# Attention's last output weights in buffers of their own, and the seventh tile's squares alone in the mean

## The chip, the core and the metric

The kernel is one program on one core of a Trainium2 chip. The metric is the device time of one launch in microseconds (us). A core has a matrix engine (PE in the profile), a vector engine (DVE), a scalar engine (ACT), a pool engine (POOL) and a queue that issues the large loads (SP). Each engine runs its instructions strictly in its own order and waits where an operand or a buffer is not ready; the engines work beside each other. Tiles live in on-chip memory of 128 partitions; matrix products go to eight accumulator banks of 512 columns.

## The reference

Two transformer layers over 256 tokens of width 1024, everything in 32-bit floats. Layer 0 mixes tokens by a mixture of three causal, dilated attentions with 16 heads, layer 1 by a gated linear attention in chunks. Both are followed by a gated feed-forward with a short convolution, and every sub-layer is normed and modulated by a conditioning vector. The part around the change:

```python
def rmsnorm(x, g):
    x32 = x.astype(jnp.float32)
    y = x32 * lax.rsqrt(jnp.mean(x32 * x32, axis=-1, keepdims=True) + EPS)
    return (y * g.astype(jnp.float32)).astype(x.dtype)
...
    return o.reshape(B, S, A_WIDTH).astype(h.dtype) @ w_out
...
        x = x + g1 * y
        h = rmsnorm(x, norm_ffn[i]) * (1.0 + sc2) + sh2
        x = x + g2 * conv_ffn(h, w_up[i], conv_w[i], conv_b[i], w_down[i])
```

## The kernel before

Activations are kept transposed: `x` is eight tiles of 128 channels by 256 tokens. Every product of 32-bit numbers is made as three products of a faster 32-bit form: each operand is split into a high part and a remainder, and `mm3` (lines 175 to 177) multiplies high by high, low by high and high by low. For a weight block `split` (line 155 on) loads the block into a raw buffer (one of four, tag `raw`), ACT rounds it to the high part `whi` in two halves (line 165), and DVE subtracts that from the raw block, again in two halves, which gives `wlo` (line 169). The pool `wspl` holds three buffers each of `whi` and `wlo`, so the fourth block in a row can be cast only when the last product that reads the first one is done.

Layer 0's attention goes over eight pairs of heads. For one pair `attend` makes the scores (tile `s`), adds the bias (`prob`, line 435), exponentiates (line 444), norms (`pn`, lines 450 and 451), transposes on PE (tile `t`, line 455), copies the result (`pt`, line 456), multiplies by the values (`po`, lines 460 and 464) and splits the result into `ohi` and `olo` (lines 469 and 470), one operand pair of 128 channels. `evacuate` takes queries and keys out of their banks (q on ACT, line 479; k on DVE, line 480).

`project` then multiplies the eight operand pairs by the output weights. It goes over four blocks n = 0 to 3 of 2048 columns; each block gives two output tiles (i = 0, 1), so 48 products `py` of 128x256. The last operand pair comes out of the last pair of heads; the products with the first seven need not wait for it. Block n has its own split weights, and the fourth one's reuse the first one's buffers. After a block `residual` adds its two tiles into `x` (DVE, line 322), `add_square` squares them on ACT (`sq`, line 199) and sums the squares (`sqacc`, line 202, tiles 0 to 2 on POOL, the rest on DVE), and `scale` makes `early_x` on ACT (line 287). `sums[0]` ends as the sum over tiles 0 to 6, `sums[1]` is tile 7 alone.

Then `all_normed` starts the feed-forward: products `early` of `early_x` with a first weight block (line 302), tiles 0 and 1 ahead of the mean; `rstd_of` multiplies `sums[0]` and `sums[1]` by a matrix of 1/1024 into one bank (tile `ms`, line 187), which is the mean over channels; ACT turns it into a reciprocal root (`ln`, `rstd`); the other six `early` products are put behind the `ms` products on PE; DVE and ACT make `xr`, `hhi` and `hlo` per tile, and PE goes on with the products `pab` of the feed-forward. The `early`, `ms`, `t` and `po` products use the slower, plain 32-bit form, and each of the first two shows as two records.

The order of the instructions on each engine is chosen when the kernel is built: a scheduler orders them by a timing model of its own under the data dependencies and buffer counts. `behind(...)` (and `issue_after`) adds an edge that keeps an instruction behind another one on the same engine. The order is fixed in the program after that; it does not react to what happens on the chip.

Of the kernel before, what the change touches and what calls it, by code (L numbers as in the profile page):

```python
# [57 lines left out]
def trunk(ctx: ExitStack, tc: tile.TileContext, I, out):  # L58
# [112 lines left out]

    def mm3(ps, a, b, start, stop):


        mm(ps, a[0], b[0], start=start, stop=False)  # L175
        mm(ps, a[0], b[1], start=False, stop=False)  # L176
        return mm(ps, a[1], b[0], start=False, stop=stop)  # L177
# [18 lines left out]
    def add_square(kt):  # L196
# [8 lines left out]
        part = 2 if kt < 3 else kt // 7  # L205
        if kt in (0, 3, 7):
            sums[part] = sq
        else:
            add(part, sq)
# [3 lines left out]
        if kt < 6:  # L213
            squared[0] = i

# [80 lines left out]
    def all_normed(l, sub, tag, early):  # L296
# [9 lines left out]
        r = rstd_of([sums[0], sums[1]], tag="p")  # L306
# [12 lines left out]
    def residual(l, sub, kt, ps):  # L319
        g = mod[l, 3 * sub + 2, kt]  # L320
        with behind(*(last_sum if kt == 7 else ())):
            i = last_x[kt // 7] = nc.vector.scalar_tensor_tensor(x[kt], ps, g[:, 0:1], x[kt], op0=ALU.mult, op1=ALU.add)
# [82 lines left out]

    def attend(u, q, k, v, bias):
# [32 lines left out]
        for h in range(2):  # L439
            rs = slice(2 * h, 2 * h + 2)  # L440
            nc.vector.tensor_scalar(m[:, 4:8][:, rs], m[:, 0:4][:, rs], -1.0, None, op0=ALU.mult)
            for r in (2 * h, 2 * h + 1):
                c = prob[r][:, 0 : KEYS + r]
                nc.scalar.activation(c, c, AF.Exp, bias=m[:, 4 + r : 5 + r], accum_out=m[:, 8 + r : 9 + r])
            nc.vector.reciprocal(m[:, 12:16][:, rs], m[:, 8:12][:, rs])
            for r in (2 * h, 2 * h + 1):
# [4 lines left out]
                nc.vector.tensor_scalar(pn[:, T:KEYS], prob[r][:, T + r : KEYS + r], f, None, op0=ALU.mult)  # L451
                t = bank("t", "t")
                for j in range(3):
                    c = slice(P * j, P * j + P)
                    nc.tensor.transpose(t[:, c], pn[:, c], ident)
                (nc.vector.tensor_copy if r % 2 else nc.scalar.copy)(pt[:, r, :], t[:, 0:KEYS])
# [4 lines left out]
        for r in range(4):  # L461
            for hh, e in enumerate(heads):
                at = P * (r % 2) + P + E * hh
                mm(po[e, CH * r : CH * r + CH], v[r // 2][:, at : at + E],
# [9 lines left out]
    def evacuate(q, k, g, pq, pk):  # L474
# [3 lines left out]
        if g:  # L478
            nc.scalar.mul(q[g], pq, 0.125)
            return nc.vector.tensor_copy(k[g], pk)  # L480
# [83 lines left out]

    def project(src, o, l, sub):
# [3 lines left out]
        for n in range(4):  # L569
            w = split(src[n], 2048)  # L570
# [6 lines left out]
            for kt, i in order:  # L577
                with behind(*(ends[n - 2 :][:1] if (n, kt) == (2, 2) else ())):
                    e = mm3(ps[i][:, T * i : T * i + T], parts(w, 2 * P * kt + P * i), o[kt],
# [4 lines left out]
            for i in range(2):  # L584
                residual(l, sub, 2 * n + i, ps[i][:, T * i : T * i + T])
                add_square(2 * n + i)
                scale(l, 1, 2 * n + i)
        return early

    early = project(I["w_out_a"], o, 0, 0)  # L590
# [5 lines left out]
    def ffn(l, early):  # L596
        w_early = [split(I["w_up"][l, 0][:, KT * P :], KT * P)]
        with behind(*sixth):
            w_early.append(split(I["w_up"][l, 1], 2048, late=last_x[1:]))
# [469 lines left out]
```

## Time and profile before

| | |
|---|---|
| median of 3 runs | 785.96 us (785.95 to 786.29) |
| profiled execution | 784.46 us, of which the span from first to last instruction is 782.7 us |
| PE busy | 769.9 us of the span (98%), 6416 products |
| DVE busy | 643.2 us (82%) |
| ACT busy | 480.2 us (61%) |
| POOL busy | 14.4 us (2%) |
| attention's last products `po` | start at 282.39 us of the span |
| first product `pab` of layer 0's feed-forward | starts at 299.91 us |

Times in rows of the trace are microseconds from the start of the span. A row of the timeline has the start, the length, the engine, the line, the operation, the output and inputs, the shape and the number of merged instructions; in square brackets at its end stands how long the engine sat idle before it, and what ended that. A row of the table by stretches has, for each engine, the busy time and the number of instructions, then the granted PE clock (1.00 is full speed), the share of time that the load engines were busy and what they moved. Products on PE are pipelined: one that is shown 0.28 us long starts 0.11 us after the one before it.

### The profile page before, as it was taken

The numbers are of one execution on the slowest core, as the hardware profiler recorded it, in microseconds if no ns is written. First come the engines' busy times: TensorE is split into PE (matmuls) and PEld (weight loads), VectorE is DVE, ScalarE is ACT, GpSimd is POOL, SyncE is SP. The second block draws the span as 40 slices with busy tenths as digits, with TensorE's granted clock in tenths as the row PEclk, the third lists the DMA queues.
The fourth block names the chain that finished last, engine by engine and source line by source line (L and its number), as shares of the span: only waits on it lengthen the run. The fifth ranks groups of instructions, "written<-read, shape, count | busy, mean of one in ns | idle before, by whom it ended". The sixth has DMA issues, their size and how long they took to land.

```text
span 782.7 us, 15883 instructions
## 1 busy us (share of the span) xinstructions
PE 769.9 (98%) x6416; PEld 741.9 (95%) x6416; DVE 643.2 (82%) x1160; ACT 480.2 (61%) x936; POOL 14.4 (2%) x40
## 2 busy tenths in 40 slices
PE   8999999999999999999999999999999999999997
PEld 6899999999999999999999999898999999999997
DVE  6998978878779758999998976797568898899762
ACT  5566555545645557867666656664667866667552
POOL 1000000000000010000000100000010000000000
PEclk9999999999999999999999999999999999999999
DMA  9998577585785736777645994966445765556741
GB/s 349 417 325 350 191 287 272 195 323 193 264 299 194 266 103 250 247 268 265 227 144 206 322 341 152 340 241 229 144 144 185 252 211 173 207 182 208 262 158 54
DMA packets 32616, 184.72 MB, mean 236 GB/s; under 512 B 5852, under 2 KB 7388, under 8 KB 16286
## 3 DMA queue, kind: packets, MB, share of 16 engines
q1 hardware_dynamic: 32160, 183.26, 65.4%
q8 instruction: 50, 0.82, 0.4%
q10 hardware_dynamic: 382, 0.45, 0.2%
q14 instruction: 24, 0.20, 0.1%
HBM read 182.59 MB, written 1.10 MB: 235 GB/s over the span
## 4 chain that ended last, share of the span: by engine, by line
PE 74%; DVE 11%; DMA 8%; ACT 4%; issue 2%; ACTq 0%; DVEq 0%
PE pab L176 10%; PE pab L175 10%; PE pab L177 10%; PE pd L177 5%; PE pd L176 5%; PE pd L175 5%; DMA raw<-in_wqk 5%; DVE wlo L169 4%; PE pqk L177 3%; PE pqk L176 3%; PE pqk L175 3%; DMA raw<-in_wv 3%; DVE ada_raw L138 2%; PE py L175 2%; PE py L177 2%
## 5 line engine op out<-in xcount | busy, mean ns | idle before, releaser
L169 DVE TENSOR_TENSOR wlo<-raw,whi 128x1024 fp32r<-128x1024 f32 (+3 forms) x274 | 291.8, 1096 | 52.5 <-ACT whi L165 51.8
L165 ACT CAST whi<-raw 128x1024 fp32r<-128x1024 f32 (+3 forms) x274 | 245.5, 945 | 135.3 <-PE pab L176 40.4
L177 PE MATMUL pab<-hhi,wlo 128*128 128x256 f32 x672 | 184.7, 276 | 0.0
L176 PE MATMUL pab<-hlo,whi 128*128 128x256 f32 x672 | 184.6, 276 | 0.0
L175 PE MATMUL pab<-hhi,whi 128*128 128x256 f32 x672 | 183.2, 277 | 0.0
L176 PEld LDWEIGHTS pab<-hlo,whi 128*128 128x128 f32 x672 | 126.0, 188 | 0.2
L177 PEld LDWEIGHTS pab<-hhi,wlo 128*128 128x128 f32 x672 | 126.1, 188 | 0.0
L175 PEld LDWEIGHTS pab<-hhi,whi 128*128 128x128 f32 x672 | 125.1, 188 | 0.1
L176 PE MATMUL pqk<-hlo,whi 128*128 128x256 f32 x440 | 123.0, 283 | 0.5 <-DVE hlo L260 0.5
L175 PE MATMUL pqk<-hhi,whi 128*128 128x256 f32 x440 | 120.5, 285 | 1.9 <-ACT hhi L259 1.4
L177 PE MATMUL pqk<-hhi,wlo 128*128 128x256 f32 x440 | 122.3, 282 | 0.0
L138 DVE CUSTOM_DVE_ANT_0 ada_raw<-ada_raw,c_bc 128x1024 f32<-128x1024 f32 x96 | 113.4, 1218 | 9.5 <-DMA ada_raw<-in_w_ada 9.5
L177 PE MATMUL pd<-ghi,wlo 128*128 128x256 f32 x352 | 97.1, 276 | 0.0
L176 PE MATMUL pd<-glo,whi 128*128 128x256 f32 x352 | 97.1, 276 | 0.0
L175 PE MATMUL pd<-ghi,whi 128*128 128x256 f32 x352 | 96.8, 276 | 0.0
L175 PEld LDWEIGHTS pqk<-hhi,whi 128*128 128x128 f32 x440 | 81.7, 190 | 3.2 <-ACT hhi L259 1.9
L176 PEld LDWEIGHTS pqk<-hlo,whi 128*128 128x128 f32 x440 | 83.3, 190 | 1.3 <-DVE hlo L260 0.9
L177 PEld LDWEIGHTS pqk<-hhi,wlo 128*128 128x128 f32 x440 | 83.1, 190 | 0.9 <-issue 0.7
L176 PEld LDWEIGHTS pd<-glo,whi 128*128 128x128 f32 x352 | 66.1, 188 | 0.0
L177 PEld LDWEIGHTS pd<-ghi,wlo 128*128 128x128 f32 x352 | 66.1, 188 | 0.0
L175 PEld LDWEIGHTS pd<-ghi,whi 128*128 128x128 f32 x352 | 65.9, 188 | 0.0
L641 ACT ACTIVATE r<-pab,small 128x256 f32<-128x256 f32 x86 | 46.7, 559 | 15.6 <-DVE r L644 15.5
(207 smaller groups left out, 1302.9 us busy)
## 6 DMA issues: line engine op xcount, KB each, us to landing
ada_raw<-in_w_ada SPq DMA_DIRECT2D x47, 1024.0 KB, 6.8
raw<-in_w_up SPq DMA_DIRECT2D x42, 1024.0 KB, 5.0
raw<-in_w_down SPq DMA_DIRECT2D x32, 704.0 KB, 4.8
raw<-in_wqk SPq DMA_DIRECT2D x18, 1024.0 KB, 7.2
raw<-in_wv SPq DMA_DIRECT2D x14, 768.0 KB, 4.5
raw<-in_w SPq DMA_DIRECT2D x7, 960.0 KB, 7.0
raw<-in_w_out_a SPq DMA_DIRECT2D x4, 1024.0 KB, 6.4
raw<-in_w_v_b SPq DMA_DIRECT2D x4, 1024.0 KB, 6.4
```

The costliest lines, as they stand in the source:

```text
L138: nc.vector.tensor_tensor_reduce(w, w, c_bc, op0=ALU.mult, op1=ALU.add, scale=1.0, scalar=0.0, accum_out=dot,)
L165: copied[0] = nc.scalar.copy(hi[:, c], raw[:, c])
L169: last_lo[0] = nc.vector.tensor_tensor(lo[:, c], raw[:, c], hi[:, c].bitcast(F32), op=ALU.subtract)
L175: mm(ps, a[0], b[0], start=start, stop=False)
L176: mm(ps, a[0], b[1], start=False, stop=False)
L177: return mm(ps, a[1], b[0], start=False, stop=stop)
L641: nc.scalar.activation(r, u[:, :T], AF.Identity, scale=cw[2], bias=col(C_CB + 44 * l + f))
```

## The change

Six things are edited, all of them in layer 0 alone except where the diff says otherwise.

1. Block n = 0 of the output weights: the first ACT cast is put behind q's evacuation and the first DVE remainder behind k's (`evacuated`), in the last pair of heads.
2. Block n = 3 goes through a new `last_out`. The weights for operand pairs 0 to 5 (1536 of 2048 columns) are split into buffers of their own in the attention's pool (`w30`, `w31`), in two pieces of 768 columns; the ACT casts are put behind the last exponential, the DVE pieces behind two given instructions of the last pair of heads. The last 512 columns go into a `wspl` buffer, in the first quarter of it. The same buffer takes the 1024 columns of the feed-forward's first block behind them (`shared`), in two pieces of 512.
3. In block n = 2 the PE order is held by three edges in place of one: operand pair 2 behind the last transpose, pair 4 behind the last `po` product, pair 5 behind the end of block 0.
4. `add_square` of tile 6 puts the squares into `sums[3]` alone; `rstd_of` gets three operands, `sums[0]` (tiles 0 to 5), `sums[3]` and `sums[1]`. One DVE sum goes away, and one `ms` product comes in its place.
5. `residual` of tile 6 is put behind the last sum on DVE, and the two `early_x` scalings of block 3 behind the square of tile 7 on ACT.
6. In `ffn` the first DVE remainder of layer 0's second block is put behind the residual of tile 7, as the second one was before.

```diff
--- before.py
+++ after.py
@@ -169,6 +169,15 @@
                 last_lo[0] = nc.vector.tensor_tensor(lo[:, c], raw[:, c], hi[:, c].bitcast(F32), op=ALU.subtract)
         return hi, lo
 
+    def split_into(pieces, high=(), low=((), ())):
+
+        for raw, hi, lo in pieces:
+            with behind(*high):
+                nc.scalar.copy(hi, raw)
+        for (raw, hi, lo), those in zip(pieces, low):
+            with behind(*those):
+                last_lo[0] = nc.vector.tensor_tensor(lo, raw, hi.bitcast(F32), op=ALU.subtract)
+
     def mm3(ps, a, b, start, stop):
 
 
@@ -193,7 +202,7 @@
 
     sums = {}
 
-    def add_square(kt):
+    def add_square(kt, alone=False):
 
         sq = tmp.tile([P, T], F32, tag="sq", name="sq")
         i = nc.scalar.activation(sq, x[kt], AF.Square)
@@ -202,8 +211,8 @@
             last_sum[:] = [(nc.gpsimd if kt < 3 else nc.vector).tensor_tensor(acc, sums[part], other, op=ALU.add)]
             sums[part] = acc
 
-        part = 2 if kt < 3 else kt // 7
-        if kt in (0, 3, 7):
+        part = 3 if alone else 2 if kt < 3 else kt // 7
+        if kt in (0, 3, 7) or alone:
             sums[part] = sq
         else:
             add(part, sq)
@@ -212,6 +221,7 @@
             sixth[1:] = last_sum
         if kt < 6:
             squared[0] = i
+        return i
 
     def shift(pool, columns):
 
@@ -303,7 +313,7 @@
                    start=(kt == 0), stop=(kt == KT - 1))
 
         products(range(2))
-        r = rstd_of([sums[0], sums[1]], tag="p")
+        r = rstd_of([sums[0], *([sums.pop(3)] if 3 in sums else []), sums[1]], tag="p")
         with behind(norm_ops[0]):
             products(range(2, KT))
 
@@ -318,7 +328,7 @@
 
     def residual(l, sub, kt, ps):
         g = mod[l, 3 * sub + 2, kt]
-        with behind(*(last_sum if kt == 7 else ())):
+        with behind(*(last_sum if kt == 7 or (l, sub, kt) == (0, 0, 6) else ())):
             i = last_x[kt // 7] = nc.vector.scalar_tensor_tensor(x[kt], ps, g[:, 0:1], x[kt], op0=ALU.mult, op1=ALU.add)
         if kt < 6:
             squared[1] = i
@@ -403,6 +413,9 @@
             ada_chunk(*rest.pop(0))
 
 
+    last_t, last_po, evacuated = [None], [None], []
+    exps, norms, turned = [], [], []
+
     def attend(u, q, k, v, bias):
 
 
@@ -441,19 +454,19 @@
             nc.vector.tensor_scalar(m[:, 4:8][:, rs], m[:, 0:4][:, rs], -1.0, None, op0=ALU.mult)
             for r in (2 * h, 2 * h + 1):
                 c = prob[r][:, 0 : KEYS + r]
-                nc.scalar.activation(c, c, AF.Exp, bias=m[:, 4 + r : 5 + r], accum_out=m[:, 8 + r : 9 + r])
+                exps.append(nc.scalar.activation(c, c, AF.Exp, bias=m[:, 4 + r : 5 + r], accum_out=m[:, 8 + r : 9 + r]))
             nc.vector.reciprocal(m[:, 12:16][:, rs], m[:, 8:12][:, rs])
             for r in (2 * h, 2 * h + 1):
 
                 f = m[:, 12 + r : 13 + r]
                 pn = att.tile([P, KEYS], F32, tag="pn", name="pn", bufs=3)
                 nc.vector.tensor_scalar(grouped(pn[:, 0:T]), by_residue(prob[r][:, 0:T]), f, None, op0=ALU.mult)
-                nc.vector.tensor_scalar(pn[:, T:KEYS], prob[r][:, T + r : KEYS + r], f, None, op0=ALU.mult)
+                norms.append(nc.vector.tensor_scalar(pn[:, T:KEYS], prob[r][:, T + r : KEYS + r], f, None, op0=ALU.mult))
                 t = bank("t", "t")
                 for j in range(3):
                     c = slice(P * j, P * j + P)
-                    nc.tensor.transpose(t[:, c], pn[:, c], ident)
-                (nc.vector.tensor_copy if r % 2 else nc.scalar.copy)(pt[:, r, :], t[:, 0:KEYS])
+                    last_t[0] = nc.tensor.transpose(t[:, c], pn[:, c], ident)
+                turned.append((nc.vector.tensor_copy if r % 2 else nc.scalar.copy)(pt[:, r, :], t[:, 0:KEYS]))
         po = bank("po", "t")
         for n in range(2):
             for hh, e in enumerate(heads):
@@ -461,7 +474,7 @@
         for r in range(4):
             for hh, e in enumerate(heads):
                 at = P * (r % 2) + P + E * hh
-                mm(po[e, CH * r : CH * r + CH], v[r // 2][:, at : at + E],
+                last_po[0] = mm(po[e, CH * r : CH * r + CH], v[r // 2][:, at : at + E],
                    pt[:, r, T + E * hh : T + E * hh + E], start=False, stop=(r == 3))
         hi = att.tile([P, T], F32R, tag=f"ohi{u}", name="ohi", bufs=1)
         lo = att.tile([P, T], F32R, tag=f"olo{u}", name="olo", bufs=1)
@@ -476,8 +489,8 @@
 
 
         if g:
-            nc.scalar.mul(q[g], pq, 0.125)
-            return nc.vector.tensor_copy(k[g], pk)
+            evacuated[:] = nc.scalar.mul(q[g], pq, 0.125), nc.vector.tensor_copy(k[g], pk)
+            return evacuated[1]
         qh, ql = q[0]
         for hh in range(2):
             own = slice(E * hh, E * hh + E)
@@ -562,12 +575,35 @@
                 next_ada()
     o = list(zip(o_hi, o_lo))
 
+    KO = 6
+
+    def last_out(src):
+
+
+        raw = wraw.tile([P, 2048], F32, tag="raw", name="raw")
+        nc.sync.dma_start(raw, src)
+        n = 2 * P * KO
+        own = [att.tile([P, n], F32R, tag=f"w3{s}", name=("whi", "wlo")[s], bufs=1)[:, :] for s in range(2)]
+        split_into([(raw[:, i : i + n // 2], own[0][:, i : i + n // 2], own[1][:, i : i + n // 2]) for i in (0, n // 2)],
+                   exps[-1:], (norms[-2:-1], turned[-3:-2]))
+        rest = [wspl.tile([P, 2048], F32R, tag=("whi", "wlo")[s], name=("whi", "wlo")[s])[:, :] for s in range(2)]
+        split_into([(raw[:, n:], rest[0][:, 0 : 2048 - n], rest[1][:, 0 : 2048 - n])])
+        shared[:] = [y[:, 2048 - n :] for y in rest]
+        return lambda kt, i: parts(own, 2 * P * kt + P * i) if kt < KO else parts(rest, 2 * P * (kt - KO) + P * i)
+
+    shared = []
+
     def project(src, o, l, sub):
 
         ends = []
         shift_columns(l, 1)
         for n in range(4):
-            w = split(src[n], 2048)
+            if l == 0 and n == 3:
+                tile_of = last_out(src[n])
+            else:
+
+                w = split(src[n], 2048, **(dict(after=(evacuated[:1], ()), low=evacuated[1:]) if n == l == 0 else {}))
+                tile_of = lambda kt, i, w=w: parts(w, 2 * P * kt + P * i)
             ps = [bank("py", "ppst"[n])] * 2
             if n == 3:
                 ps[1] = bank("py", "s")
@@ -575,18 +611,27 @@
             if n == 3:
                 order.sort(key=lambda x: x[1])
             for kt, i in order:
-                with behind(*(ends[n - 2 :][:1] if (n, kt) == (2, 2) else ())):
-                    e = mm3(ps[i][:, T * i : T * i + T], parts(w, 2 * P * kt + P * i), o[kt],
+
+                first = {(2, 2): last_t, (2, 4): last_po, (2, 5): ends[:1]} if l == 0 else {(2, 2): ends[:1]}
+                with behind(*first.get((n, kt), ())):
+                    e = mm3(ps[i][:, T * i : T * i + T], tile_of(kt, i), o[kt],
                             kt == 0 and (n == 3 or i == 0), kt == KT - 1 and (n == 3 or i == 1))
             ends.append(e)
             if n == 3:
                 early = load_early(I["w_up"][l, 0])
             for i in range(2):
                 residual(l, sub, 2 * n + i, ps[i][:, T * i : T * i + T])
-                add_square(2 * n + i)
-                scale(l, 1, 2 * n + i)
+                squared_now = add_square(2 * n + i, alone=(l, n, i) == (0, 3, 0))
+                if (l, n) != (0, 3):
+                    scale(l, 1, 2 * n + i)
+            if (l, n) == (0, 3):
+
+                with behind(squared_now):
+                    for i in range(2):
+                        scale(l, 1, 2 * n + i)
         return early
 
+    shift(att, 8)
     early = project(I["w_out_a"], o, 0, 0)
     at_pool.__exit__(None, None, None)
 
@@ -594,9 +639,15 @@
     last_pd = [None]
 
     def ffn(l, early):
-        w_early = [split(I["w_up"][l, 0][:, KT * P :], KT * P)]
+        if l == 0:
+            raw = wraw.tile([P, 2048], F32, tag="raw", name="raw")
+            nc.sync.dma_start(raw[:, 0 : KT * P], I["w_up"][l, 0][:, KT * P :])
+            split_into([(raw[:, c : c + 512], shared[0][:, c : c + 512], shared[1][:, c : c + 512]) for c in (0, 512)])
+            w_early = [shared]
+        else:
+            w_early = [split(I["w_up"][l, 0][:, KT * P :], KT * P)]
         with behind(*sixth):
-            w_early.append(split(I["w_up"][l, 1], 2048, late=last_x[1:]))
+            w_early.append(split(I["w_up"][l, 1], 2048, low=() if l else last_x[1:], late=last_x[1:]))
         h, whole = all_normed(l, 1, "s", early)
         with tc.tile_pool(name=f"ffn{l}", bufs=2) as pool:
             shift(pool, 16)
```

Beside these, eight columns of padding are added to the attention's pool (`shift(att, 8)`).

## The prediction

> **What bounds the kernel now.** I read the page first, then the table by stretches, then PE's timeline around the change, then ACT's and DVE's.
>
> ```profile
> span 782.7 us, 15883 instructions
> PE 769.9 (98%) x6416; PEld 741.9 (95%) x6416; DVE 643.2 (82%) x1160; ACT 480.2 (61%) x936; POOL 14.4 (2%) x40
> ```
> ```profile
> 278.00:286.00 8.00, 6.80 (x68) 6.12 (x68) 2.39 (x6) 1.67 (x4) 0.00 (x0) 1.00 0.00 1
> 286.00:295.60 9.60, 9.60 (x87) 9.60 (x86) 8.50 (x16) 9.33 (x20) 2.40 (x2) 1.00 0.48 173
> ...
> 300.00:440.00 140.00, 140.00 (x1234) 139.88 (x1233) 130.28 (x229) 98.45 (x184) 0.80 (x1) 1.00 0.68 236
> ```
>
> PE is the bound: it is busy in 98% of the span, and without a gap from 300 to 440. So what PE loses or gains by 300 us arrives at the end. The stretch 278 to 286 has 1.20 us without PE work. The next one is the row to remember: in those 9.60 us ACT is busy for 9.33, almost as full as PE.
>
> ```profile
> 261.69 0.62 PE L417 MATMUL s<-k,q 128*128 128x258 f32 x3
> 262.24 0.33 PE L424 MATMUL s<-k,q 64*64 64x64 f32 x4
> 263.15 0.45 PE L175 MATMUL pv<-whi,hhi 128*128 128x384 f32 x1 [0.58 <-DVE k L480]
> ...
> 281.16 0.49 PE L455 MATMUL t<-ident,pn 128*128 128x128 f32 x3
> 282.39 1.08 PE L460 MATMUL po<-pt,v 128*64 128x256 f32 x8 [0.74 <-DVE pt L456]
> 283.27 0.66 PE L464 MATMUL po<-pt,v 128*64 128x64 f32 x16
> 284.40 0.50 PE L175 MATMUL py<-ohi,whi 128*128 128x256 f32 x2 [0.46 <-ACT ohi L469]
> ...
> 288.14 0.28 PE L175 MATMUL py<-ohi,whi 128*128 128x256 f32 x1
> 288.25 0.28 PE L176 MATMUL py<-olo,whi 128*128 128x256 f32 x1
> ...
> 295.62 1.03 PE L302 MATMUL early<-early_x,raw 128*128 128x257 f32 x4
> 296.49 0.59 PE L187 MATMUL ms<-sqacc,ones_d 128*128 128x256 f32 x2
> 296.96 0.70 PE L187 MATMUL ms<-sq,ones_d 128*128 128x256 f32 x2
> 297.50 2.76 PE L302 MATMUL early<-early_x,raw 128*128 128x257 f32 x12
> ```
>
> PE waits three times: 0.58 us for k, 0.74 for the last `pt`, 0.46 for `ohi`. A `py` product takes 0.113 us (288.14 to 288.25). The mean is just in time: `ms` on tile 7's squares starts at 296.96, and PE goes on at 297.50.
>
> ```profile
> 259.32 2.00 ACT L165 CAST whi<-raw 128x1024 fp32r<-128x1024 f32 x2 [1.86 <-DMA raw<-in_w_out_a]
> ...
> 285.66 3.05 ACT L165 CAST whi<-raw 128x1024 fp32r<-128x1024 f32 x4 [1.32 <-PE py L176]
> 288.61 0.41 ACT L199 ACTIVATE sq<-x_all 128x256 f32<-128x256 f32 x1
> ...
> 292.54 0.40 ACT L199 ACTIVATE sq<-x_all 128x256 f32<-128x256 f32 x1
> 292.85 0.49 ACT L287 ACTIVATE early_x<-x_all,mod 128x256 f32<-128x256 f32 x1
> 293.25 1.98 ACT L165 CAST whi<-raw 128x1024 fp32r<-128x1024 f32 x2
> 295.13 0.41 ACT L199 ACTIVATE sq<-x_all 128x256 f32<-128x256 f32 x1
> 295.45 0.49 ACT L287 ACTIVATE early_x<-x_all,mod 128x256 f32<-128x256 f32 x1
> 296.50 0.42 ACT L199 ACTIVATE sq<-x_all 128x256 f32<-128x256 f32 x1 [0.55 <-DVE x_all L322]
> ```
>
> This is the chain that the mean hangs on. At 285.66 the first block's products are done and free its buffer; ACT casts the fourth block and half of the feed-forward's first (2.95 us), then six squares and scalings (to 293.25), then two casts for the feed-forward's second block (1.88 us), then the squares of tiles 6 and 7. Its only slack ahead of the last square is the 0.55 us.
>
> **The change part by part.** *Evacuation first (edit 1).*
>
> ```profile
> 260.40 2.36 DVE L169 TENSOR_TENSOR wlo<-raw,whi 128x1024 fp32r<-128x1024 f32 x2 [2.20 <-ACT whi L165]
> 262.68 0.42 DVE L480 COPY k<-pqk 128x256 f32<-128x256 f32 x1
> ```
>
> With one remainder (1.14 us) in place of two ahead of it, k starts at 261.54 and the second `pv` at 262.0 instead of 263.15. In the changed program the scores at 261.69 (0.8 us with their four small products) no longer stand ahead of `pv` but after it, so PE gains 1.15 - 0.8 = 0.3 us. What is queued behind k on DVE, two modulation reductions, comes sooner by as much; the delayed remainder follows them, near 265.4, and `py`, which reads it, comes only after the 24 `pv` products.
>
> ```profile
> raw<-in_w_out_a SPq DMA_DIRECT2D x4, 1024.0 KB, 6.4
> ```
>
> Block 3's load waits on SP for the raw buffer that this remainder frees: 265.4, not 262.8. With 6.4 us from issue to landing it is there by 272, ahead of the last exponential, behind which its casts stand.
>
> *The fourth block early (edits 2, 3).* The two casts of 768 columns fall after the last exponential (ACT is idle there until the first `pt`), the two remainders into DVE's gaps among the `pn`: so transposes and ACT's waits for PE cover them, at no cost; uncovered they would put off `pt` by less than the 2.00 us of two whole casts. In the built order PE does 25 more `py` products ahead of `po` than before (121, not 96): 25 x 0.113 = 2.8 us. So `po` starts at 262.0 + (281.65 - 263.15) + 2.8 + 0.8 = 284.1, and the last transposes stand 26 products ahead of it, so that `pt` is long done: the wait of 0.74 goes. After `po` come 23 other products, so `ohi` is ready too and the 0.46 goes. With the restarts after these waits PE ends its last `py` about 2 us earlier in its work. One of the plain `early` products is put among the `py`; that costs two changes of form, 0.2 us.
>
> *What is late next.* Those 23 products stand ahead of the last operand pair's products with blocks 0 and 1. Block 0 ended at 285.66 before. Now `po` ends at 285.5 and the last product that reads block 0's `whi` is the 32nd after it: 285.5 + 0.1 + 31 x 0.113 + 0.28 = 289.4. On that product the first of the three ACT casts of 512 columns waits (its buffer is block 0's), and on ACT everything stands behind that cast: all eight squares, the scalings, the two 1024 casts. So ACT starts this chain 3.8 us later and does less in it: 2.95 - 1.88 = 1.07 us is two casts of 512, so three are 1.6 in place of 2.95. The first square starts at 289.45 + 1.6 = 291.05, 2.4 later than 288.61. The rest is the same work in the same order: the two casts at 295.7, tile 6's square at 297.55, tile 7's (no wait for `x` is left, it is ready by 297) from 297.86 to 298.27.
>
> ```profile
> 292.97 0.43 DVE L202 TENSOR_TENSOR sqacc<-sqacc,sq 128x256 f32<-128x256 f32 x1 [0.28 <-ACT sq L199]
> ```
>
> *PE meets it.* After `po` 71 `py` are left: 285.6 + 71 x 0.113 = 293.65, with two plain `early` products and their changes PE reaches the mean at 294.75. The sum over tiles 0 to 5 hangs on ACT's sixth square (292.54 + 2.4): DVE's two sums after it (0.43 each) end at about 296.1, and PE waits 1.4 us. One `ms` product, 0.43, and PE waits another 1.4 for tile 6's square. Then two `ms`: PE goes on at 298.85, not 297.50.
>
> *Squares alone (edits 4 to 6).* The extra `ms` product is 0.43 us on PE, and it is in that sum; the DVE sum saved (0.42) hides behind ACT. Scaling after squares takes 0.4 us from tile 7's square and gives it to `early_x`, which PE needs 1.7 us after the mean. The feed-forward's remainder behind the residual waits for its cast anyway. The raw buffer behind block 3 frees some 2 us later, near 292; a load issued then has landed by 298.4, ahead of the first `pab`. POOL's two sums move with ACT's squares.
>
> Sum so far: 298.85 - 297.50 = +1.35 us, say 1.4. PE has gained 2 us and idled 2.8.
>
> *The clock.* The idle is new in kind: 2.8 us in a stretch of 3.3, with 0.43 of work inside.
>
> ```profile
> 10.87 1.47 PE L374 MATMUL rows<-oh,tab 33*16 33x512 f32 x6
> ```
> ```profile
> 10.30:13.70 3.40, 2.83 (x17) 1.62 (x16) 2.14 (x5) 3.37 (x8) 0.00 (x0) 1.00 1.03 422
> 13.70:17.10 3.40, 3.40 (x17) 3.40 (x17) 3.40 (x5) 1.18 (x5) 0.00 (x0) 0.50 1.03 427
> ```
>
> Here the granted clock fell to 0.50 for a stretch of 3.4 us, right after one in which PE idled 0.57 and worked 1.47 on products of 33 rows by 16 columns; 1.20 of idle in the 8 us from 278 did not bring it down (the next row has 1.00). If narrow products count for little, about 2 us of 3.4 without work is enough and 1.2 is not. The new idle has 1.4 to 2.8 in any stretch of 3.4, by where the edges fall. So I take it that one stretch at half clock follows. It costs half of what of it lies after PE's restart at 298.0: 1.1 us if it began at 296.8, 1.7 if at 298 or later. On the edges of this trace (13.7 + 83 x 3.413 = 297.0) it is 1.2; I take 1.4, between the ends. In all +2.8 us: 784.46 + 2.8 = 787.3 for the profiled execution. That one lies 1.5 us under the median, so the forecast on the median is 785.96 + 2.8 = 788.8.
>
> **The rivals.** *The clock stays.* Then +1.4 remains: 787.4, at the edge of what can be told from no change (0.2%, 1.6 us). For it: the waits around 282 did not change the clock. Against it: they came to 1.2 us, not to 2.8. The Trainium skill ("TensorE: Matmul & The Clock Gate", "What's actually happening" and "HAM oscillation") says that the clock halves after at least one idle window of about 3.4 us, and asks for no idle gaps above that; by that rule nothing happens here, since a product lies between two waits of 1.4. The trace agrees with its window of 3413 ns, but not with the need for a wholly idle one: PE was busy 2.83 of 3.40 ahead of its fall.
>
> *Faster: ACT keeps up.* If ACT's chain were not behind, PE would keep its 2 us less 0.3 for the third `ms` (0.43 less part of the wait in the 0.70 us row): 784.3. It is one place, tile 7's square: it must end by 296.9, 1.3 us sooner than I have it, and all ahead of it is a fixed row of ACT work from 289.4 on. It would take the two 1024 casts (1.88) standing behind the squares, and they stand ahead.
>
> *Little change.* The chain starts up to 1 us earlier than worked out, by a shorter way to block 0's last product: +0.4, the idle falls under 2 us and the clock holds: 786.4. Against it: each term is a row.
>
> **How the numbers follow.** Forecast 0.56 (own range 787.9 to 789.5); clock stays 0.26; little change 0.08; faster 0.06; above 789.5, two slow stretches or a stall of the feed-forward behind the late buffers, 0.04. The range 786.4 to 789.5 leaves out 0.06, 0.04 and half of the 0.08. Faster by over 0.2%: 0.06. Slower by over 0.2% (from 787.53): 0.54 of the forecast, a third of the second case, 0.04 above: 0.66. The rest, 0.28, within.
>
> **What would show it.** Right: PE's waits for `pt` and `ohi` gone; `po` near 284; ACT's cast of 512 columns waiting for `py` until about 289.4; PE idle twice, about 1.4 us each, ahead of `ms`, for `sqacc` and for `sq`; a stretch of 3.4 us at clock 0.50 behind that; `pab` starting 1.4 us later than 299.91 or more. Wrong: `ms` by 296.5, or ACT's squares starting before 290; no idle on PE ahead of `ms`; the clock at 1.00 throughout, which is the first rival.

## The result, and the profile after

The changed kernel takes 789.2 us (median of 7 runs, 786.83 to 792.64) against 786.15 (7 runs, 785.68 to 787.94): 1.0045 times the kernel before, 95% interval 1.003 to 1.006. It is slower, by about 3.5 us by this ratio (2.4 to 4.7 by the interval; the two medians differ by 3.05). The forecast was +2.8 us.

The profiled execution took 789.2 us. Head of its page, then its table by stretches (columns as before: PE, PEld, DVE, ACT and POOL busy, granted clock, load engines).

```profile
span 787.4 us, 15887 instructions
...
PE 770.8 (98%) x6418; PEld 742.0 (94%) x6418; DVE 644.5 (82%) x1160; ACT 480.2 (61%) x937; POOL 13.8 (2%) x40
```
```profile
278.00:286.00 8.00, 8.00 (x73) 7.59 (x73) 2.94 (x6) 0.96 (x2) 0.00 (x0) 1.00 0.02 4
286.00:295.60 9.60, 9.60 (x93) 9.23 (x89) 5.29 (x11) 5.40 (x14) 1.81 (x2) 1.00 0.19 53
295.60:300.00 4.40, 2.00 (x8) 1.28 (x8) 4.08 (x7) 4.31 (x9) 0.00 (x0) 0.97 0.93 328
300.00:304.00 4.00, 4.00 (x14) 3.25 (x12) 3.04 (x9) 2.56 (x6) 0.00 (x0) 0.61 0.78 279
304.00:308.00 4.00, 4.00 (x36) 3.97 (x34) 4.00 (x9) 3.72 (x9) 0.00 (x0) 1.00 0.72 248
```

From 278 to 295.6 PE now has no gap, which the kernel before did not manage. ACT, busy for 9.33 of the 9.60 us from 286 before, is busy for 5.40: it waits for PE. From 295.6 to 300 it is the other way round: ACT is full (4.31 of 4.40) and PE works 2.00. Then the granted clock is 0.61 on the mean of four microseconds.

PE's timeline around the mean, and ACT's:

```profile
285.05 1.08 PE L473 MATMUL po<-pt,v 128*64 128x256 f32 x8
...
295.16 0.60 PE L312 MATMUL early<-early_x,raw 128*128 128x257 f32 x2
297.18 0.70 PE L196 MATMUL ms<-sqacc,ones_d 128*128 128x256 f32 x2 [1.42 <-DVE sqacc L211]
298.85 1.29 PE L196 MATMUL ms<-sq,ones_d 128*128 128x256 f32 x4 [0.98 <-ACT sq L208]
299.94 4.33 PE L312 MATMUL early<-early_x,raw 128*128 128x257 f32 x12
303.92 0.59 PE L184 MATMUL pab<-hhi,whi 128*128 128x256 f32 x2
```
```profile
290.53 1.66 ACT L176 CAST whi<-raw 128x512 fp32r<-128x512 f32 x3 [3.51 <-PE py L185]
292.10 0.41 ACT L208 ACTIVATE sq<-x_all 128x256 f32<-128x256 f32 x1
...
296.51 1.97 ACT L165 CAST whi<-raw 128x1024 fp32r<-128x1024 f32 x2
298.39 0.72 ACT L208 ACTIVATE sq<-x_all 128x256 f32<-128x256 f32 x2
```

PE reaches the mean at 295.76 and waits 1.42 us for the sum and 0.98 for tile 6's square. The 12 records of `early` behind it take 3.98 us (299.94 to 303.92); before they took 2.41 (297.50 to 299.91). On ACT, the cast of 512 columns waited 3.51 us for a `py` product, and everything else stands behind it.

All profiled executions, cut at the same four instructions (differences of the start times of rows): the first `py`, the third `early` product (PE's restart behind the mean), the first `pab`, the first `pab` on `lv` (a copy of two operand tiles that the feed-forward's fifth weight block reads), the end of the span. In e5 the third column holds 1.89 us of added products, in e12 a wait of 1.73 us.

| run | first `py` to restart | restart to `pab` | `pab` to `lv` | `lv` to end | clock 0.50 near 300 |
|---|---|---|---|---|---|
| kernel before | 29.48 | 2.41 | 23.48 | 459.27 | no |
| changed kernel | 31.20 | 3.98 | 24.22 | 459.29 | 299.69 to 303.11 |
| e9_after_look | 31.45 | 3.64 | 24.22 | 461.62 | 298.37 to 301.78 |
| e10_after_look | 31.09 | 2.41 | 23.49 | 459.49 | no |
| e1_order / e8_order_again | 28.93 / 28.84 | 2.41 | 23.49 | 459.28 / 460.72 | no |
| e2_warm | 31.09 | 2.41 | 23.49 | 459.29 | no |
| e7_warm2 / e11_warm2_look | 30.99 / 31.10 | 2.41 | 24.37 | 459.31 / 461.92 | no |
| e3_sum7 | 32.90 | 4.22 | 24.21 | 459.30 | 296.76 to 303.59 |
| e4_evac | 29.59 | 2.41 | 23.50 | 459.23 | no |
| e5_pitch | 28.94 | 4.30 | 23.22 | 461.81 | no |
| e6_order_sum7 | 29.87 | 2.41 | 24.37 | 459.29 | no |
| e12_casts_late | 30.22 | 4.49 | 24.54 | 459.30 | no |

So the profiled pair differs by 4.75 us of span as follows: 0.55 before the first scores (64.92 against 64.37, ahead of anything that was changed), 0.16 from there to the first `py` (203.81 against 203.65), 1.72 by the stall, 1.57 in the `early` products at half clock, 0.74 from `pab` to `lv`, 0.02 from there to the end.

### The profile page after: what moved, and what is told of

Read it like the earlier page. It is cut to its first block, busy times and chain, and to the rows that moved or that the text cites. A ratio compares the mean times of both kernels' runs of the same rounds, so it can differ in the third digit from the quotient of the medians.

```text
span 787.4 us, 15887 instructions
## 1 busy us (share of the span) xinstructions
PE 770.8 (98%) x6418; PEld 742.0 (94%) x6418; DVE 644.5 (82%) x1160; ACT 480.2 (61%) x937; POOL 13.8 (2%) x40
## 4 chain that ended last, share of the span: by engine, by line
PE 73%; DVE 11%; DMA 8%; ACT 4%; issue 2%; ACTq 0%; DVEq 0%
PE pab L184 10%; PE pab L186 10%; PE pab L185 10%; PE pd L184 5%; PE pd L186 5%; PE pd L185 5%; DMA raw<-in_wqk 5%; DVE wlo L169 5%; PE pqk L186 3%; PE pqk L185 3%; PE pqk L184 3%; DMA raw<-in_wv 2%; DVE ada_raw L138 2%; PE py L184 2%; PE py L185 2%
## 5 line engine op out<-in xcount | busy, mean ns | idle before, releaser
L169 DVE TENSOR_TENSOR wlo<-raw,whi 128x1024 fp32r<-128x1024 f32 (+4 forms) x270 | 288.5, 1099 | 54.9 <-ACT whi L165 54.2
L165 ACT CAST whi<-raw 128x1024 fp32r<-128x1024 f32 (+4 forms) x270 | 242.4, 945 | 136.3 <-PE pab L185 41.6
```

Of the source, the lines that this page charges most:

```text
L165: copied[0] = nc.scalar.copy(hi[:, c], raw[:, c])
L169: last_lo[0] = nc.vector.tensor_tensor(lo[:, c], raw[:, c], hi[:, c].bitcast(F32), op=ALU.subtract)
```

## The experiments

Every run computes all that the reference asks; the runs e2, e5, e7 and e11 make some products more, whose results nothing reads. Times are compared by the ratio to the kernel before on the same chip.

**Is the order on PE the cause of the stall?** The changed kernel with block 0's last products moved up:

```diff
-                first = {(2, 2): last_t, (2, 4): last_po, (2, 5): ends[:1]} if l == 0 else {(2, 2): ends[:1]}
+                first = {(2, 2): last_t, (2, 4): ends[:1]} if l == 0 else {(2, 2): ends[:1]}
+                if (l, n, kt, i) == (0, 3, 0, 0):
+                    first[3, 0] = ends[:1]
```

> The changed kernel with another order on PE: after the last po product come five products of block 3's second tile and then at once the last operand pair's products with blocks 0 and 1; block 2's pairs from 4 on and block 3's first tile are held behind block 0's end. Nothing else is changed. So block 0's last read of whi is the 9th product after po and not the 32nd. Theory (the ACT chain starts late because block 0's buffer comes free late): ACT's cast of 512 columns moves from 290.5 to about 288, all squares come 2.4 us earlier, PE's two waits ahead of ms (1.4 and 1.0) shrink to 0.6 in all or less, no stretch at half clock follows, the early products take 2.4 us and not 4.0: 784.5 to 785.8, faster than the changed kernel by 3 to 4.5 us and at or under the kernel before. Rival (the waits ahead of ms come from the new order of residuals, squares and scalings, not from the start of the chain): ACT's casts move but PE still waits 1.5 us or more ahead of ms, and the time stays above 787.5.

Measured: 785.46 us, 0.999 of the kernel before (0.9981 to 1.000), and in a second set (e8_order_again) 784.59, again 0.999 (0.998 to 0.9999); I had 785.5 for that one.

> The kernel of the run e1_order once more, beside e6_order_sum7 on the same chip. Theory: 0.6 us faster than the kernel before, 785.5, with no wait over 0.3 us on PE between 272 and 300. Rival (the order wins nothing over the kernel before): 786.1.

ACT's and PE's timelines of e1_order:

```profile
287.81 1.66 ACT L176 CAST whi<-raw 128x512 fp32r<-128x512 f32 x3 [1.34 <-PE py L185]
289.37 0.41 ACT L208 ACTIVATE sq<-x_all 128x256 f32<-128x256 f32 x1
...
295.68 0.72 ACT L208 ACTIVATE sq<-x_all 128x256 f32<-128x256 f32 x2
```
```profile
295.48 0.59 PE L196 MATMUL ms<-sqacc,ones_d 128*128 128x256 f32 x2
296.15 1.13 PE L196 MATMUL ms<-sq,ones_d 128*128 128x256 f32 x4
297.11 2.76 PE L312 MATMUL early<-early_x,raw 128*128 128x257 f32 x12
```

ACT starts 2.7 us earlier (the profiled execution as a whole is 0.55 earlier at the first `py`), both waits are gone (0.24 us of the second is left in e8_order_again), so is the half clock, and the kernel is about 4 us faster than the changed one by the ratios; against the kernel before it is between no change and 0.2% faster. The edit is on PE alone, and up to the mean ACT and DVE do the same in the same order in both traces: the stall comes from what PE's order puts ahead of block 0's last read, on which ACT's cast waits. Behind 303 us, in the feed-forward, the built order of ACT and DVE is another too (e1_order has that of the kernel before there). That costs nothing visible: from `lv` to the end both kernels take 459.3 us.

**Could ACT keep up if its casts stood elsewhere?** The changed kernel with the two 1024 casts behind tile 7's square:

```diff
+                sixth[:1] = [squared_now]
                 with behind(squared_now):
                     for i in range(2):
```

> The changed kernel with the two 1024 casts of the feed-forward's second block held behind tile 7's square on ACT instead of ahead of tile 6's; PE's order stays. They then stand ahead of ln and rstd, and their two remainders on DVE ahead of the first xr. Theory (ms hangs on ACT's chain, and the casts are 1.9 us of it; the first wait, for the sum over tiles 0 to 5, stays): the wait for sq shrinks from 1.0 us to 0.3 or less, the early products start 30.0 to 30.4 us after the first py and not 31.2; but ln comes after the casts, so hhi comes late and PE waits 2 us or more ahead of pab: the first pab 35 us or more after the first py, 788.5 to 790.5 in all. Rival (the casts do not hold the squares up: these wait for the residuals anyway): the restart stays at 31.2. Rival (ACT keeps up once the casts are out of the way): first pab by 33 us, 787 or less.

Measured: 790.72 us, 1.0066 (1.0043 to 1.0089). Its PE timeline:

```profile
296.27 0.70 PE L196 MATMUL ms<-sqacc,ones_d 128*128 128x256 f32 x2 [1.33 <-DVE sqacc L211]
297.17 1.13 PE L196 MATMUL ms<-sq,ones_d 128*128 128x256 f32 x4 [0.20 <-ACT sq L208]
298.14 2.76 PE L312 MATMUL early<-early_x,raw 128*128 128x257 f32 x12
302.63 0.50 PE L184 MATMUL pab<-hhi,whi 128*128 128x256 f32 x2 [1.73 <-ACT hhi L269]
```

Nearly as expected: the restart comes 1.0 us earlier, and a wait of 1.73 us for `hhi` (I had 2 or more) takes its place; the first `pab` comes 34.71 us after the first `py` (I had 35 or more), and the time is just above the range. Shifting these two casts behind the squares does not help; ACT has to start earlier.

**Are stall and clock two losses?** The changed kernel with five products to fill PE's first wait (`fill` holds the instruction that they stand behind, the second `early` product, and their number, five in layer 0's feed-forward):

```diff
+        for _ in range(fill[1]):
+            with behind(last):
+                last = mm(ps[:, T : T + P], ones_d, ones_d, start=True, stop=True)
...
```

> The changed kernel with five more plain products of 128x128 (constant operands, into columns of the mean's bank that nothing reads) between the second early product and the first ms product, where PE waited 1.4 us. They take about 1.6 us, so they put off the first ms product by 0.2 us and the restart behind tile 7's square by nothing. Theory (stall and clock are two losses): the stall stays, so the early products still start near 299.9 of the span, but the idle left is 1 us or less, the granted clock stays at 1.00, the early products take 2.4 us and not 4.0, and PE reaches pab while hhi and hlo are still being made: 1.6 us less from the clock, and 0.7 less if the longer pitch of the pab products (0.118 and not 0.113 us until 328) goes with it: 787.0 to 788.0 where the changed kernel has 789.3. Rival (the half clock does not come from the idle ahead of ms): a stretch at 0.50 is there all the same, and the time is that of the changed kernel, 789 to 790.

Measured: 788.47 us, 1.0031 (1.002 to 1.0043). PE's timeline, and the stretch with the remaining idle:

```profile
296.21 1.27 PE L198 MATMUL ms<-ones_d 128*128 128x128 f32 x10
297.79 0.70 PE L201 MATMUL ms<-sqacc,ones_d 128*128 128x256 f32 x2 [0.30 <-DVE sqacc L216]
299.47 1.13 PE L201 MATMUL ms<-sq,ones_d 128*128 128x256 f32 x4 [0.98 <-ACT sq L213]
300.43 2.76 PE L317 MATMUL early<-early_x,raw 128*128 128x257 f32 x12
```
```profile
298.13:301.54 3.41, 2.43 (x12) 1.84 (x11) 2.66 (x3) 3.26 (x8) 0.00 (x0) 1.00 0.62 259
```

The stall is what it was (31.09), the half clock is gone and the `early` products take 2.41 us again: in this trace the two are separate losses of 1.6 us each. The time, though, fell by less than expected, and its interval overlaps that of the changed kernel. So the second wait was filled too, with three more products:

```diff
+            for _ in range(3 if fill[1] and i == 0 else 0):
+                with behind(last):
+                    last = mm(ps[:, T : T + P], ones_d, ones_d, start=False, stop=False)
...
```

> The kernel of the run e2_warm with three more such products between the first and the second ms product, where PE still waited 1.0 us. So the stall is as long as in the changed kernel, but PE idles in no more than 0.7 us of it. Theory (the half clock follows from idle time in a window of 3.4 us; 1.9 or more brought it, 1.4 or less did not): the clock stays at 1.00 around 300 in every execution, PE starts the early products 31.1 to 31.3 us after its first py product as in the changed kernel, then 23.5 us from first pab to first lv: 787.5 to 788.2, the same as e2_warm or up to 0.5 less. Rival (the clock falls by something else than idle time): a half clock near 300 in this run too, 789 or more.

> The kernel of e7_warm2 profiled once more, since its times ran from 786.6 to 793.7 us while its first profiled execution showed no half clock near 300. Theory (idle time brings the fall): no half clock near 300 in this execution either; where it is slow, by the longer pitch or by a late load. Rival (the plain 128x128 products do not count as work, so the clock can fall in spite of them): in a slow execution a half clock near 300, first py to first pab 35 us.

Measured: 789.74 us, 1.005 (1.0032 to 1.0069), no better than the changed kernel, and well above what I expected. The profiled executions (787.62 and 790.89 us) both have the clock at 1.00 near 300, stall 30.99 and 31.10, `early` 2.41. They differ elsewhere. Their tables by stretches, e7_warm2 and then e11_warm2_look, the same program:

```profile
742.00:746.00 4.00, 4.00 (x38) 4.00 (x37) 2.44 (x4) 1.93 (x4) 0.04 (x1) 1.00 1.01 355
770.00:774.00 4.00, 4.00 (x38) 4.00 (x37) 0.00 (x0) 0.00 (x0) 0.00 (x0) 1.00 0.00 0
```
```profile
742.00:746.00 4.00, 4.00 (x36) 4.00 (x35) 3.77 (x5) 2.04 (x4) 0.00 (x0) 1.00 1.01 378
770.00:774.00 4.00, 4.00 (x36) 4.00 (x36) 1.69 (x2) 0.77 (x2) 0.00 (x0) 1.00 0.02 4
```

With the granted clock at 1.00, no gap on PE and nearly no transfers at 770, one execution has 38 products in the 4 us and the other 36 (a row counts those that reach in from before; 36 and 34 start there, 0.113 and 0.118 us apart). From the first `lv` product to the end they take 459.31 and 461.92 us. That is 2.6 us by which executions of one program differ, 0.73 of it a wait for `wlo` at 740.02, most of the rest the pitch; it has nothing to do with the change.

Whether the filler keeps the clock up in every execution is not shown. Three were profiled with filler, and none fell near 300. But four of the ten timed executions of e7_warm2, the four from 790.83 to 793.66 us, have a mean granted clock of 0.995, and the 26 of the kernel before beside e2_warm have 0.996 to 1.000. One more stretch of 3.41 us at 0.50 takes 0.002 off the mean. So in these four the clock probably fell once more than in the others; where, no trace shows.

**What lengthens the stretch from `pab` to `lv`?** e1_order with eight products ahead of `pab`:

```diff
+        for _ in range(8 if l == 0 else 0):
+            with behind(last):
+                last = mm(mean[0][:, T : T + P], ones_d, ones_d, start=True, stop=True)
...
```

> The kernel of the run e1_order with eight more plain products of 128x128 (constant operands, results unread) on PE between the last early product and the first pab, about 1.75 us of work, so that the first hhi and hlo are done before PE asks for them. The granted clock should stay at 1.00 here. In the runs so far the pab products up to the first one that reads lv took 23.5 us where PE had waited briefly for the first hhi and hlo (kernel before, e1_order, e2_warm, e4_evac), and 24.2 us where it came late behind a half clock (changed kernel, e3_sum7). Theory (the longer pitch, 0.118 instead of 0.113 us, comes from PE meeting no wait there, and not from the clock): from first pab to first lv 24.2 us here too, so 1.75 + 0.7 = 2.4 us more than e1_order, 787.9. Rival (the longer pitch is an after-effect of the half clock): 23.5 us, and 1.75 us more, 787.2.

Measured: 787.95 us, 1.0035 (1.002 to 1.005); 23.22 us from `pab` to `lv`. My theory fell: without any wait there the pitch is the short one. The rival does not hold either, since e6, e7, e11 and e12 have 24.4 to 24.5 us with the clock at 1.00. What sets the pitch stays open.

**What are the edits 4 and 5 worth?** The changed kernel, and e1_order, without them:

```diff
-                squared_now = add_square(2 * n + i, alone=(l, n, i) == (0, 3, 0))
+                squared_now = add_square(2 * n + i, alone=False)
-                if (l, n) != (0, 3):
-                    scale(l, 1, 2 * n + i)
-            if (l, n) == (0, 3):
-
-                with behind(squared_now):
-                    for i in range(2):
-                        scale(l, 1, 2 * n + i)
+                scale(l, 1, 2 * n + i)
...
-        with behind(*(last_sum if kt == 7 or (l, sub, kt) == (0, 0, 6) else ())):
+        with behind(*(last_sum if kt == 7 else ())):
```

> The changed kernel without its last edits: tile 6's squares go into the sum over tiles 0 to 6 again (one ms product less, one DVE sum more behind tile 6's square), the residual of tile 6 is not held behind the last sum, and the scalings are not held behind tile 7's square. Theory (these edits cost and gain next to nothing; the late start of ACT's chain is the cause): ACT's cast of 512 columns still waits until 290.5, PE waits about as long ahead of ms as with the edits (2 to 3 us in one or two waits), the half clock follows as before: 788.7 to 790.3, within 1 us of the changed kernel. Rival (the mean in three parts is what costs): the waits ahead of ms fall under 1 us and the time to 787 or less.

> The kernel of the run e1_order with tile 6's squares in the sum over tiles 0 to 6 again, and without the two edges on the residual and the scalings (as in e3_sum7). Theory (with ACT's chain early, the mean in three parts saves a wait of about 1 us for the sum behind tile 6's square and costs 0.43 us for its product): PE waits about 1 us for sqacc ahead of ms, restarts 0.5 to 0.7 us later than in e1_order, too little for a half clock: 785.9 to 786.3 against 785.5. Rival (the third product is only a cost when ACT is early): 0.4 us faster than e1_order, 785.0.

Measured: e3_sum7 790.84 us, 1.0059 (1.0047 to 1.0071); e6_order_sum7 786.12, 1.0009 (0.9998 to 1.002), against 784.59 and 0.999 (0.998 to 0.9999) of e8_order_again beside it. Rows of e3_sum7:

```profile
298.02 1.22 PE L196 MATMUL ms<-sqacc,ones_d 128*128 128x256 f32 x2 [3.95 <-DVE sqacc L211]
299.03 1.11 PE L196 MATMUL ms<-sq,ones_d 128*128 128x256 f32 x2
```
```profile
293.35:296.76 3.41, 0.71 (x5) 0.31 (x3) 1.91 (x5) 3.37 (x7) 0.15 (x1) 1.00 0.99 372
296.76:300.17 3.41, 2.15 (x5) 1.57 (x6) 2.63 (x4) 1.56 (x5) 0.00 (x0) 0.50 0.38 156
300.17:303.58 3.41, 3.41 (x9) 2.67 (x9) 2.90 (x8) 2.20 (x5) 0.00 (x0) 0.50 0.59 168
```

Without the split mean PE waits once, for 3.95 us (I had 2 to 3), restarts 1.7 us later, and the clock stays down for two windows. About 0.9 us of the 1.7 is the clock: the `ms` products themselves run at half of it, and from the first of them to the restart pass 1.92 us, where the kernel before took 1.01. In e1_order's order the wait for the sum is 0.96 us and the restart 1.0 us later. So the squares alone are a gain of 0.8 to 1.0 us of stall; they are not the cause.

**Edit 1 alone**, on the kernel before:

```diff
-            w = split(src[n], 2048)
+            w = split(src[n], 2048, **(dict(after=(evacuated[:1], ()), low=evacuated[1:]) if n == l == 0 else {}))
...
```

> The kernel before with edit 1 alone: block 0's first cast behind q's evacuation, its first remainder behind k's. Theory: k is ready 1.1 us earlier, PE gains 0.3 us net, nothing later is late: 0.2 to 0.5 us faster than the kernel before, so 785.5 to 785.9. Rival (block 3's load, which then starts 2.6 us later, is late for its casts, or py waits for the delayed remainder): a wait of PE for wlo near 268 or of ACT for the raw block, and 786.5 or more.

Measured: 785.5 us, 0.9992 (0.998 to 1.0004): not told from no change by the time. In the trace PE's wait for k is gone, and the first `py` comes 203.10 us after the first scores, not 203.65.

**The changed kernel twice more**, to see what each execution has:

> The changed kernel itself, profiled once more, to see which parts of its loss are there in every execution. Theory: the stall of 1.7 us ahead of ms is there every time; the half clock behind it only where 1.9 us or more of the idle falls into one window of 3.4 us, about every second time by where the windows' edges fall; the longer pitch behind it by chance. So the first pab product starts 33.5 us after the first py product without the half clock and 35.2 with it (31.9 in the kernel before). Rival: all three are there every time, 35.2 us and 24.2 us on to the first lv product.

> The changed kernel once more, as in e9_after_look; the same two expectations.

Measured: 790.56 and 786.24 us. The stall is in all three executions (31.20, 31.45, 31.09). The half clock is in two, and the first `pab` comes 35.18, 35.09 and 33.50 us after the first `py`, as the theory has it. Tables by windows of 3.41 us, with the edges at which the clock changes in each trace: the first execution, e9 and e10.

```profile
296.28:299.69 3.41, 1.53 (x6) 1.06 (x7) 3.38 (x6) 3.41 (x7) 0.00 (x0) 1.00 0.95 322
299.69:303.10 3.41, 3.41 (x10) 2.68 (x9) 2.45 (x6) 2.42 (x6) 0.00 (x0) 0.50 0.70 231
```
```profile
294.95:298.36 3.41, 1.18 (x4) 0.75 (x5) 3.10 (x7) 3.41 (x7) 0.00 (x0) 1.00 0.95 375
298.37:301.78 3.41, 3.41 (x9) 2.71 (x9) 2.10 (x5) 2.21 (x6) 0.00 (x0) 0.50 0.59 178
```
```profile
293.96:297.37 3.41, 1.75 (x10) 0.94 (x8) 2.95 (x8) 3.36 (x8) 0.48 (x1) 1.00 1.02 394
297.37:300.78 3.41, 2.68 (x12) 2.39 (x13) 2.60 (x4) 2.71 (x8) 0.00 (x0) 1.00 0.73 221
```

The waits are nearly the same each time, 1.3 to 1.4 and 1.0 us; only the windows' edges lie differently. Where one window holds 1.88 or 2.23 us of idle, the next is at half clock. In e10 an edge divides the waits into 1.66 and 0.73, and the clock stays. How much idle it takes is not settled by this. In the changed kernel's first execution another window, 81 steps of 3.413 us ahead of the one that ends at 299.69, has 1.86 us of idle, and the clock stays at 1.00 behind it:

```profile
19.80:23.20 3.40, 1.54 (x10) 1.46 (x10) 3.40 (x5) 1.51 (x3) 0.00 (x0) 1.00 1.03 415
23.20:26.60 3.40, 2.92 (x25) 2.80 (x24) 3.40 (x7) 1.64 (x4) 0.00 (x0) 1.00 1.03 398
```

## Why the prediction was right or wrong

The direction, the mechanism of the stall and its place were right. The size was short: +2.8 us forecast, about +3.5 measured; 1.0045 times the 786.15 of all runs before is 789.7, just above the range's upper end of 789.5. The step that failed is the last one of the sum, what comes behind the first `pab`, which it put at nothing; beside it the sum counts the fall of the clock in full, and one execution of three has none. By the steps:

- *Evacuation first, -0.3.* Alone it is worth 0.55 us in its stage (e4_evac). In the changed kernel's first profile it gave nothing (+0.16):

```profile
260.36 1.05 ACT L165 CAST whi<-raw 128x1024 fp32r<-128x1024 f32 x1 [1.98 <-DMA raw<-in_w_out_a]
```

```profile
263.06 0.45 PE L184 MATMUL pv<-whi,hhi 128*128 128x384 f32 x1 [0.47 <-DVE k L492]
```

  The first cast waited for its load until 260.36, and PE still waited 0.47 us for k. I had k 1.1 us earlier because I held the start of the first remainder fixed; it hangs on a load, and that lands at another time in each execution. In e4_evac, where PE did not wait:

```profile
259.05 1.05 ACT L165 CAST whi<-raw 128x1024 fp32r<-128x1024 f32 x1 [1.37 <-DMA raw<-in_w_out_a]
```

  In e9 and e10, where the cast starts at 259.48 and 259.62, the first `py` comes 202.83 and 203.13 us after the first scores, 0.82 and 0.52 less than before. On the mean of the three executions the step is worth about what was forecast.

- *Casts and remainders covered, the waits for `pt` and `ohi` gone, `po` at 284.1.* Right: no such wait is left, and `po` starts at 285.05, of which 0.71 is the later first `py` (268.73 against 268.02).

- *What is late next: the cast of 512 columns at 289.4, first square at 291.05.* Right: 290.53 and 292.10, or 289.8 and 291.4 without that 0.71.

- *PE meets it: waits of 1.4 and 1.4, +1.35 us.* The waits are 1.42 and 0.98; the second is shorter because the first `ms` product holds PE for 0.70 us and not 0.43. From the first `py` on, the forecast was 1.35 + 0.3 = 1.65 us; measured 1.72, 1.97 and 1.61, of which 0.12 and 0.45 in the first two are `ms` products that already run at half clock (from the second `ms` row to the restart 1.09 and 1.42 us, 0.97 in e10). Right. e1_order shows that the late read of block 0 is the cause, which until then was only argued.

- *The clock: one stretch at half clock, 1.4 (1.1 to 1.7).* Right in size where it falls: 1.57 and 1.23 us behind the restart, with the part in `ms` 1.7 both times. But it is not in every execution, and the sum had it as a fixed term. The ground for it was weak too. The prediction took products of 33 rows by 16 columns for little work, and so counted about 2 us without work ahead of the fall at 13.70. In e4_evac a window holds the same products (1.47 us) and 0.86 us of idle, 2.33 in all, and the clock stays:

```profile
9.29:12.70 3.41, 2.55 (x14) 1.39 (x13) 2.34 (x5) 2.60 (x6) 0.00 (x0) 1.00 1.05 423
12.70:16.11 3.41, 3.20 (x24) 2.92 (x25) 3.22 (x4) 1.83 (x5) 0.00 (x0) 1.00 1.01 418
```

  So that the fall came as forecast was in part luck.

- *What the sum lacks.* The sum ends at the first `pab`. It takes a `py` or `pab` product as 0.113 us throughout and puts what follows at nothing, since what PE loses by 300 us arrives at the end. In the three executions of the changed kernel what follows costs 0.76, 3.09 and 0.23 us against the profile of the kernel before: 0.74, 0.74 and 0.01 from `pab` to `lv`, where the pitch is 0.118 us in the first two, and 0.02, 2.35 and 0.22 from `lv` to the end. With the clock at 1.7, 1.7 and 0 us, one program gives spans that lie 4.76, 6.12 and 1.79 us above the one profile of the kernel before. Whether the change brings the longer pitch is not shown. The kernel before has a stretch of it too (27 products from 268.24 to 271.42), it has a single profile, 1.5 us under its median, and one program showed both pitches at one place (e9 and e10). So where the difference between 2.8 and about 3.5 comes from stays open; the interval of 2.4 to 4.7 us holds both.

Of the rivals, "the clock stays" is what e10 did: a stall of 1.61 us and no fall. It took 786.24 us, where the rival had 787.4; a single execution of the kernel before beside it took 786.26. "Faster: ACT keeps up" named its condition, tile 7's square done by 296.9 and 784.3 us in all; e1_order meets it (the two squares end at 296.40) and takes 785.46 and 784.59. But the way named there, casts behind the squares, is not the way (e12_casts_late).

The Trainium skill ("TensorE: Matmul & The Clock Gate", "What's actually happening") lets the clock fall after at least one idle window of about 3.4 us. The traces do not bear out that the window has to be idle: PE worked 1.53 and 1.18 us of the 3.41 ahead of the falls above. The same section says that the window runs freely and does not start with the kernel; with that the traces agree, since equal waits brought the fall at 299.69, at 298.37 or not at all.

## What to carry to other kernels

When a change gives a tile buffers of its own, look for the buffer that still is shared, find the last instruction that reads it in the built order, and count what the new order puts ahead of that instruction: here 23 products (2.6 us) started ACT's chain so late that the new waits cost more than the two that went. Before a mean or any other narrow meeting point, add up the idle that falls within one stretch of 3.4 us; in these traces 1.88 us in one window was enough to pay the stall twice, though 1.86 in another was not. And cut several traces at the same instructions before explaining a difference of 1 us: single executions of one program differed by more, at places that the change never touched.

## What the hardware showed that I had not expected

The same 128x256 product has two pitches at a granted clock of 1.00, 0.113 and 0.118 us (36 and 34 starts in 4 us), and keeps the longer one for anything from 3 us (kernel before, 268.24 to 271.42) to 64 (e9_after_look, 564 to 628). e7_warm2 and e2_warm met the same short waits at the first `pab` and came out with 24.37 and 23.49 us to `lv`. It was tied neither to the half clock (e6, e7, e11, e12) nor to the lack of a wait (e5). The Trainium skill (the page named above, "Wait — 56ns, not 53.3ns?") has one fixed cost per product beside its columns; the second pitch is not in it.

The clock fell near 300 after windows with 1.88, 2.23 and 2.70 us of idle, and not after 1.66, 1.24 (e12_casts_late, 298.73 to 302.14), 1.17 (e6_order_sum7, 295.22 to 298.63) and 0.98 (e2_warm). Near the start of the program, counted from the edges at which the clock changes, windows with 2.01 (e1_order, 19.07 to 22.48) to 2.48 us (e11_warm2_look, 18.34 to 21.75) brought a fall in eight executions, and 1.73 (e4_evac, 19.53 to 22.94) and 1.86 (the changed kernel) did not. Idle alone does not settle it: the kernel before fell after 0.57 (10.30 to 13.70), and in e5_pitch 1.93 us brought no fall (779.92 to 783.33, at the end of the program). In e3_sum7 it stayed down for a second window in which PE worked 2.15 of 3.41 us.
